# Second layer's input projection by seven block products of summed operands in place of eight, in a two-layer fp32 trunk on one core

## The chip, the core and the metric

The kernel runs on one core of a Trainium2 chip. The core has a matrix engine (PE, TensorE; its weight loads are listed as PEld), a vector engine (DVE), a scalar engine (ACT), a third elementwise engine (POOL, GpSimd) and a queue that issues transfers (SP). Each engine takes its instructions in the order in which they stand; semaphores hold one engine until another is done. SBUF holds operands in 128 partitions; PE writes to PSUM, which has eight banks of 512 fp32 columns.

The metric is the device time of one execution in microseconds (us). Three runs of the kernel before took 918.66, 919.13 and 919.36 us; the median is 919.13.

## The reference

Two residual layers over 512 tokens of 1024 channels, in fp32. The first (even) layer has mLSTM heads and stick-breaking attention; the change leaves what it computes alone. The second (odd) layer is this:

```python
def odd_layer(x, pre_g, post_g, w_in, pool_w, pool_scale, w_out):
    h = rmsnorm(x, pre_g)
    u = h @ w_in                                   # (512, 1024) @ (1024, 4096)
    p, z = u[..., :2048], u[..., 2048:]
    pooled = multiscale_pool(p in 4 groups)        # windows 2, 4, 8, 16
    mixed = einsum('bsgc,gce->bsge', pooled, pool_w) * pool_scale
    y = (mixed * silu(z)) @ w_out
    return x + rmsnorm(y, post_g)
```

The change is in `h @ w_in`.

## The kernel before

**Exact products in three.** PE multiplies in a reduced fp32 form, so every operand is cut in two exact parts: `split` (L70) writes the high half on ACT and the low half, source minus high half, on DVE. A product is then three matmuls, high by high, high by low and low by high (`mm3`, L93). The normed tokens stand transposed as `hTh` and `hTl`, 128 channels by 8 by 512 tokens.

**The odd layer** (L624 to L729) goes through four groups, one for each window (2, 4, 8, 16). For a group it loads the weights of four column tiles of p, 256 columns to a transfer (`col_load`), splits each tile's weights (1024 elements a partition) and multiplies: `col_proj` (L188) runs 8 channel blocks by 3 matmuls of 128x512 for each tile. Group 0 does this in two halves of 256 tokens, since the last tokens of the first layer come late. ACT copies each result out of PSUM; DVE forms window sums (L684), divides, subtracts (L689 to L691) and splits the result into `pph` and `ppl`. Then follow four column tiles of z (`project2`, with Silu on the way out into `sz`), and the group's 512 by 512 map `mx` (L706), whose result DVE scales and multiplies by `sz` into `y32`. After the fourth group comes the output projection `oq` (L537).

**What sets the order.** The program is written in the order above and a scheduler of the framework interleaves it: it chooses each engine's order when the program is built, from its own estimate of durations. Buffers come from rings: `w32` (2 buffers, weights as they come), `wh` and `wl` (4 each, their halves), PSUM banks `pj`, `sc`, `ac` (2 each), `xa` and `xb` (1 each). A ring's next buffer is free when the last reader of its old content is done.

**Names in this text.** `p20` is the first pair of column tiles of p in group 2, `z21` the second pair of z there, `pw` a group's map weights, `mx` its products. `finish_even` (L640) ends the first layer for a tile of 128 tokens and makes the odd layer's normed tokens of it (`prenorm`, L161).

Of the kernel before, what the change touches and what calls it, by code (L numbers as in the profile page):

```python
# [5 lines left out]
F32 = mybir.dt.float32  # L6
# [7 lines left out]
P = 128  # L14
S = 512
# [21 lines left out]
def body(nc, tc, x, pre_g, post_g, w_in, conv, b_i, b_f, hn_g, w_out, w_in_c, pool_w,  # L37
# [6 lines left out]
    with base as base, psum as psum, dram as dram:  # L44
# [10 lines left out]
        # functions that need a table run in the order they are written, so that each  # L55
        # table is loaded once for a run of them
# [21 lines left out]
        def load(parts, a, n, name):  # L78
            """Weights as they come, rows of n columns for each of a row tiles."""
            w32 = base.tile([P, 8 * WIDE // 4], F32, tag="w32", bufs=2, name=f"w32_{name}")  # L80
            w = w32[:, :a * n].rearrange("p (a n) -> p a n", a=a)
            for eng, dst, src in parts(w):
                eng.dma_start(dst, src.rearrange("(a p) n -> p a n", p=P))
            return w

        def halves(w, name, into=None):
            """The two exact parts of a piece of them."""
            a, n = w.shape[1], w.shape[2]
            wh, wl = (t[:, :a * n].rearrange("p (a n) -> p a n", a=a) for t in (into or whl(name)))
            split(w, wh, wl)  # L90
            return wh, wl
# [13 lines left out]
        # the first layer's input and gate rows stand where its output goes later  # L105
# [8 lines left out]
        # constants  # L114
# [21 lines left out]
        # per-channel vectors, one transpose  # L136
# [24 lines left out]
        def prenorm(xt, xs, tt, gain, name, parts=1):  # L161
            ss = base.tile([P, 1], F32, tag="ss", bufs=4, name=f"ss_{name}")
            if parts == 1:
                A.activation(xs, xt, AF.Square, accum_out=ss)
            else:
                s2 = base.tile([P, 2], F32, name=f"s2_{name}")
                for n in range(2):
                    cs = slice(n * 512, n * 512 + 512)
                    A.activation(xs[:, cs], xt[:, cs], AF.Square, accum_out=s2[:, n:n + 1])
                V.tensor_tensor(ss, s2[:, 0:1], s2[:, 1:2], op=ALU.add)  # L170
            r = rstd(ss, name)
            for half in range(2):
                hs = slice(half * 512, half * 512 + 512)
                V.scalar_tensor_tensor(xs[:, hs], xt[:, hs], r, gain[:, hs], op0=ALU.mult,
                                       op1=ALU.mult)
                tp = sc(f"tp{half}_{name}")
                for j in range(4):
                    k = half * 4 + j
                    T.transpose(tp[:, j * P:(j + 1) * P], xs[:, k * P:(k + 1) * P], ident)
                dst = (slice(None), slice(half * 4, half * 4 + 4), slice(tt * P, tt * P + P))  # L180
                split(tp.rearrange("p (a n) -> p a n", a=4), hTh[dst], hTl[dst])

        def col_load(src, name):
            """Two column tiles of an input projection."""
            w = load(lambda t: [(nc.sync, t, src)], 8, 256, name)
            return [lambda i=i: halves(w[:, :, i * P:i * P + P], f"{name}_{i}") for i in range(2)]
# [12 lines left out]
        with tc.tile_pool(name="att", bufs=1) as at:  # L199
# [11 lines left out]
            # first pre-norm, and the values of four heads as its tokens come  # L211
# [206 lines left out]
            class Stick:  # L418
                """One head of stick-breaking attention, key blocks from the last to the first."""
# [120 lines left out]
            def y_split(half, c, tiles, name):  # L540
                """Two channel tiles of y, for one half of the tokens."""
# [82 lines left out]
        with tc.tile_pool(name="odd", bufs=1) as od:  # L624
            def gains(g, name):
                t = od.tile([P, D], F32, tag="gain", bufs=2, name=name)
# [3 lines left out]
            def xs(name): return od.tile([P, D], F32, tag="xs", bufs=2, name=name)  # L630

            def ytiles(n):
                return (od.tile([P, S], F32R, tag="phi", bufs=6, name=f"yh_{n}"),
                        od.tile([P, S], F32R, tag="plo", bufs=6, name=f"yl_{n}"))
# [5 lines left out]
            def finish_even(ps, tt):  # L640
                xt = od.tile([P, D], F32, tag="xt", bufs=2, name=f"xe{tt}")
                nc.sync.dma_start(xt, xr[:, tt])
                t = xs(f"xse{tt}")
                post(ps, t, gpo, xt, xn[:, tt], f"e{tt}")
                prenorm(xn[:, tt], t, tt, gpr, f"p1{tt}")
# [7 lines left out]
            gpo1 = gains(post_g[1], "g_post1")  # L653
            for g, w in enumerate(WINDOWS):
                pooled = []
                cur4 = []
                for j in range(4):
# [4 lines left out]
                wj = [w for i in range(2)  # L662
                      for w in col_load(w_in_c[0, :, 512 * g + 256 * i:512 * g + 256 * i + 256], f"p{g}{i}")]
                if g == 0:
                    wj = [w() for w in wj]
                    steps = [(j, wj[j], n) for n in range(2) for j in range(4)]
                else:
                    steps = [(j, wj[j], None) for j in range(4)]
                for j, wt, n in steps:
                    wt = wt() if n is None else wt  # L670
                    n0, n1 = (0, S) if n is None else (256 * n, 256 * n + 256)
                    ps = pj(f"ps_p{4 * g + j}_{n}")
                    col_proj(wt, ps, n0, n1)
                    A.activation(cur4[j][:, 16 + n0:16 + n1], ps[:, n0:n1], AF.Copy)
                for j in range(4):
# [17 lines left out]
                    ph = od.tile([P, S], F32R, tag="phi", bufs=6, name=f"pph{c}")  # L693
                    pl = od.tile([P, S], F32R, tag="plo", bufs=6, name=f"ppl{c}")
# [3 lines left out]
                for j, ps in enumerate(p for i in range(2) for p in project2(  # L698
                        w_in_c[0, :, 2048 + 512 * g + 256 * i:2304 + 512 * g + 256 * i], f"z{g}{i}")):
                    c = 4 * g + j  # L700
                    t = od.tile([P, S], F32, tag="sz", bufs=6, name=f"sz{c}")
                    act(t, ps, AF.Silu)
                    sz.append(t)
# [10 lines left out]

            outr = out[0].rearrange("(a p) d -> p a d", p=P)

            def finish_odd(ps, tt):
                t, q = xs(f"xo{tt}"), od.tile([P, D], F32, tag="xt", bufs=2, name=f"xq{tt}")
# [37 lines left out]
```

## Time and profile before

| what | value |
|---|---|
| median of three runs | 919.13 us |
| span of the profiled execution, first to last instruction (the only time recorded of that execution) | 916.9 us |
| mean granted PE clock | 0.994 |
| first z product to first `oq` matmul | 621.8 to 814.85 us |
| output projection of the odd layer | to 910 us |
| the last rows of the odd layer behind it | 910 to 916.9 us |

A row of the grouped views reads: line, engine, operation, output <- inputs by the program's names, partitions x elements, count | busy us and mean ns of one | idle time of the engine before it and what ended it. A row of the timeline reads: start, duration, engine, line, operation; in brackets the idle time before it and its releaser. A row of windows reads: stretch and its length, then busy time (and count) by engine, the granted clock of PE as a share of full speed, the share of time in which transfers ran, and GB/s.

### The profile page before, as it was taken

What the parts mean: (1) busy time and instruction counts of PE and PEld (TensorE: products, weight loads), DVE (VectorE), ACT (ScalarE), POOL (GpSimd) and SP (SyncE); (2) the same over time, 40 slices, a digit from 0 to 9 for tenths busy, and PEclk for the clock granted to TensorE, in tenths of its full rate; (3) what the DMA queues carried; (4) which work ended last, traced back from release to release, by engine and by line L of the source; (5) the groups of instructions that cost most, each with busy time, mean ns of one, the idle gap of its engine ahead of it and who ended that gap; (6) DMA issues with size and microseconds to landing.
All of it is one profiled execution on the core that took longest, in us unless ns stands there. A gap on an engine that the chain in (4) does not pass through costs nothing.

```text
span 916.9 us, 11439 instructions
## 1 busy us (share of the span) xinstructions
PE 904.5 (99%) x4453; PEld 759.6 (83%) x4453; DVE 533.8 (58%) x817; ACT 461.5 (50%) x766; POOL 51.9 (6%) x189
## 2 busy tenths in 40 slices
PE   8999999999999999999999999999999999999996
PEld 6788889889988898898898878898888888888885
DVE  5435556567876675764764828665462745737542
ACT  6426666766668464464565536553231422335331
POOL 2001111101101101001000000000000000000000
PEclk8999999999999999999999999999999999999999
DMA  8231321212122332324221456624223333326331
GB/s 299 84 101 49 91 85 54 88 51 82 59 92 90 129 93 95 98 78 133 92 87 52 158 183 229 204 78 136 92 91 93 92 92 92 98 87 229 114 115 47
DMA packets 67126, 98.88 MB, mean 108 GB/s; under 512 B 2848, under 2 KB 54136, under 8 KB 67072
## 3 DMA queue, kind: packets, MB, share of 16 engines
q1 hardware_dynamic: 65888, 98.08, 32.9%
q8 instruction: 35, 0.57, 0.3%
q10 hardware_dynamic: 1184, 0.08, 0.1%
q14 instruction: 19, 0.16, 0.1%
HBM read 96.02 MB, written 2.13 MB: 107 GB/s over the span
## 4 chain that ended last, share of the span: by engine, by line
PE 97%; DMA 1%; DVE 1%; ACT 0%; issue 0%; DVEq 0%; POOL 0%; POOLq 0%
PE op L537 10%; PE oq L537 10%; PE ps_z L97 3%; PE ps_qa L97 3%; PE ps_qa L95 3%; PE ps_qa L96 3%; PE ps_z L95 3%; PE ps_z L96 3%; PE ps_p_None L96 2%; PE ps_p_None L95 2%; PE ps_p_None L97 2%; PE psv_va L95 2%; PE psv_va L97 2%; PE psv_va L96 2%; PE ps_zb L95 2%; PE mx L97 2%
## 5 line engine op out<-in xcount | busy, mean ns | idle before, releaser
L97 PE MATMUL ps_qa<-hTh,wl_qa 128*128 128x512 f32 x128 | 50.3, 393 | 0.0
L95 PE MATMUL ps_qa<-hTh,wh_qa 128*128 128x512 f32 x128 | 50.2, 393 | 0.0
L97 PE MATMUL ps_z<-hTh,wl_z 128*128 128x512 f32 x128 | 50.2, 393 | 0.0
L96 PE MATMUL ps_qa<-hTl,wh_qa 128*128 128x512 f32 x128 | 50.2, 392 | 0.0
L95 PE MATMUL ps_z<-hTh,wh_z 128*128 128x512 f32 x128 | 50.2, 392 | 0.0
L96 PE MATMUL ps_z<-hTl,wh_z 128*128 128x512 f32 x128 | 50.2, 392 | 0.0
L71 ACT ACTIVATE wh_p<-w_p 128x1024 fp32r<-128x1024 f32 x16 | 17.0, 1059 | 60.9 <-PE mx L96 31.9
L72 DVE TENSOR_TENSOR wl_wo_e<-w_wo_e,wh_wo_e 128x1024 fp32r<-128x1024 f32 x28 | 34.2, 1232 | 21.9 <-ACT wh_wo_e L71 21.9
L71 ACT ACTIVATE wh_wo_e<-w_wo_e 128x1024 fp32r<-128x1024 f32 x28 | 29.3, 1058 | 30.3 <-DMA w_wo_e<-in_w_out_ab 15.6
L72 DVE TENSOR_TENSOR wl_p<-w_p,wh_p 128x1024 fp32r<-128x1024 f32 x16 | 19.6, 1223 | 35.1 <-ACT wh_p L71 35.1
L537 PE MATMUL op<-wl_wo_e,yh_e 128*128 128x512 f32 x120 | 39.0, 396 | 0.0
L537 PE MATMUL op<-wh_wo_e,yl_e 128*128 128x512 f32 x120 | 38.8, 395 | 0.0
L537 PE MATMUL op<-wh_wo_e,yh_e 128*128 128x512 f32 x120 | 37.8, 396 | 0.0
L95 PE MATMUL ps_p_None<-hTh,wh_p 128*128 128x512 f32 x96 | 37.7, 393 | 0.0
L96 PE MATMUL ps_p_None<-hTl,wh_p 128*128 128x512 f32 x96 | 37.7, 393 | 0.0
L97 PE MATMUL ps_p_None<-hTh,wl_p 128*128 128x512 f32 x96 | 37.7, 392 | 0.0
L67 ACT ACT_TABLE_LOAD x28 | 35.9, 1283 | 1.3 <-PEq L742 0.8
L97 PE MATMUL psv_va<-wh_va,hTl 128*128 128x256 f32 x128 | 36.1, 282 | 0.0
L95 PE MATMUL psv_va<-wh_va,hTh 128*128 128x256 f32 x128 | 36.1, 282 | 0.0
L96 PE MATMUL psv_va<-wl_va,hTh 128*128 128x256 f32 x128 | 36.1, 282 | 0.0
L317 DVE SCALAR_TENSOR_TENSOR cv<-u,vecs,cv 128x511 f32<-128x511 f32 (+2 forms) x48 | 35.4, 748 | 0.4
L72 DVE TENSOR_TENSOR wl_wo_o<-w_wo_o,wh_wo_o 128x1024 fp32r<-128x1024 f32 x20 | 24.2, 1223 | 18.9 <-ACT wh_wo_o L71 18.9
(310 smaller groups left out, 2659.7 us busy)
## 6 DMA issues: line engine op xcount, KB each, us to landing
w_wo_e<-in_w_out_ab SPq DMA_DIRECT2D x14, 1024.0 KB, 4.9
w_wo_o<-in_w_out_c SPq DMA_DIRECT2D x12, 1024.0 KB, 4.7
w_qa<-in_w_in_ab SPq DMA_DIRECT2D x8, 1024.0 KB, 5.0
w_p<-in_w_in_c SPq DMA_DIRECT2D x8, 1024.0 KB, 5.4
w_z<-in_w_in_c SPq DMA_DIRECT2D x8, 1024.0 KB, 5.4
w_qb<-in_w_in_ab SPq DMA_DIRECT2D x4, 1024.0 KB
w_kb<-in_w_in_ab SPq DMA_DIRECT2D x4, 1024.0 KB, 5.0
w_zb<-in_w_in_ab SPq DMA_DIRECT2D x4, 1024.0 KB, 4.9
```

The source lines that it names most:

```text
L67: link(A.preload_act_table_set(TABLE[func]))
L71: A.activation(hi, src, AF.Copy)
L72: V.tensor_tensor(lo, src, hi.bitcast(F32), op=ALU.subtract)
L95: T.matmul(dst, lhsT=ah, rhs=bh, start=first, stop=False, **kw)
L96: T.matmul(dst, lhsT=ah, rhs=bl, start=False, stop=False, **kw)
L97: T.matmul(dst, lhsT=al, rhs=bh, start=False, stop=last, **kw)
L317: V.scalar_tensor_tensor(acc[:, j:], u[:, :S - j], cw(3 - j, c), acc[:, j:], op0=ALU.mult, op1=ALU.add)
L537: T.matmul(ps[a][n], lhsT=l[:, ta], rhs=r[:, 0, n * 512:n * 512 + 512], start=(first and l is yh and r is wh), stop=(last and l is yl))
```

## The change

A pair of column tiles (256 columns of `w_in`) and the 512 tokens are cut in two by two blocks: channels 0 to 511 and 512 to 1023, first and second column tile, tokens 0 to 255 and 256 to 511. Eight block products become seven, by Strassen's scheme in Winograd's form:

- `hidden_sums` forms four combinations of token blocks once (`d3`, `d1`, `n2`, `t4`, each 128x1024, on DVE) and splits each. They need the normed tokens unsplit, so `prenorm` now also copies each transposed tile into `y32` (ACT, 128x512, eight copies).
- `strassen2` forms four sums of weight blocks for each pair (`s1` to `s4`, each 128x512, on POOL), and splits `a` (first column tile, 1024), `b` and `c` (the sums, 1024 each) and `d` (the fourth weight block, 512). Each of seven products is 4 channel blocks by 3 matmuls of 128x256.
- Partial results are added where they are made: PSUM bank `psa` runs on through four products and is read after each (`pt1`, `pt2`, an output, an output), `pse` through two, `psb` holds one. Three of the reads are copies on ACT, three are additions on DVE, the last is an ACT copy or Silu.
- Group 0's p tiles stay as they were; 14 pairs use the scheme (z of group 0, p and z of groups 1 to 3).
- Rings: gains, squares and input tiles share one ring `big` of 8 with the split token sums; `phi`, `plo` 5 in place of 6, `sz` 4 in place of 6, a new ring `ws` of 3 for the sums; the last gain is loaded after the groups. Two small window operations go from DVE to POOL.

```diff
-        def prenorm(xt, xs, tt, gain, name, parts=1):
+        def prenorm(xt, xs, tt, gain, name, parts=1, keep=None):
...
-                split(tp.rearrange("p (a n) -> p a n", a=4), hTh[dst], hTl[dst])
+                tp = tp.rearrange("p (a n) -> p a n", a=4)
+                split(tp, hTh[dst], hTl[dst])
+                if keep is not None:
+                    A.activation(keep[:, half * 4:half * 4 + 4], tp, AF.Copy)
...
+            def quarter(k, n): return y32[:, 8 * n + 4 * k:8 * n + 4 * k + 4, 0:256]
+            hs = {"11": hblock(0, 0), "21": hblock(1, 0), "22": hblock(1, 1)}
+            def ws(name): return od.tile([P, 8, P], F32, tag="ws", bufs=3, name=name)
+            def hidden_sums():
+                raw = {}
+                b11, b21, b12, b22 = quarter(0, 0), quarter(1, 0), quarter(0, 1), quarter(1, 1)
+                for n in ("d3", "d1", "n2", "t4"):
...
+                    if n == "d3":
+                        V.tensor_tensor(raw[n], b22, b12, op=ALU.subtract)
+                    elif n == "d1":
+                        V.tensor_tensor(raw[n], b11, b12, op=ALU.subtract)
+                    elif n == "n2":
+                        V.scalar_tensor_tensor(raw[n], raw["d3"], -1.0, b11, op0=ALU.mult, op1=ALU.subtract)
+                    else:
+                        V.scalar_tensor_tensor(raw[n], raw["n2"], -1.0, b21, op0=ALU.mult, op1=ALU.subtract)
+                    split(raw[n], *hs[n])
+            def strassen2(src, name, dsts, silu=False):
+                w = load(lambda t: [(nc.sync, t, src)], 8, 256, name)
+                a11, a12, a21, a22 = (w[:, 4 * k:4 * k + 4, m * P:m * P + P]
+                                      for m in range(2) for k in range(2))
+                sums = [ws(f"ws{i}_{name}") for i in range(2)]
+                s1, s2, s3, s4 = sums[0][:, 4:], sums[0][:, :4], sums[1][:, :4], sums[1][:, 4:]
+                G.tensor_tensor(s1, a21, a22, op=ALU.add)
+                G.tensor_tensor(s2, s1, a11, op=ALU.add)
+                G.tensor_tensor(s3, a11, a21, op=ALU.add)
+                G.tensor_tensor(s4, a12, s2, op=ALU.add)
+                first = halves(w[:, :, :P], f"{name}_a")
+                second = halves(sums[0], f"{name}_b")
+                third = halves(sums[1], f"{name}_c")
+                fourth = halves(a22, f"{name}_d")
...
+                pa, pb, pe = (f(f"ps{n}_{name}")[:, :256] for f, n in ((pj, "a"), (xa, "b"), (xb, "e")))
+                product(pa, first, 0, "11", True, True)
+                A.activation(t1, pa, AF.Copy)
+                product(pb, first, 4, "21", True, True)
+                V.tensor_tensor(dsts[0][:, :256], pb, t1, op=ALU.add)
+                product(pa, second, 0, "n2", False, True)
+                A.activation(t2, pa, AF.Copy)
+                product(pe, second, 4, "d1", True, True)
+                A.activation(t5, pe, AF.Copy)
+                product(pa, third, 0, "d3", False, True)
+                V.scalar_tensor_tensor(dsts[1][:, 256:], pa, -1.0, t5, op0=ALU.mult, op1=ALU.subtract)
+                product(pe, third, 4, "22", False, True)
+                V.tensor_tensor(dsts[0][:, 256:], pe, t2, op=ALU.add)
+                product(pa, fourth, 0, "t4", False, True)
...
-                    V.tensor_tensor(sm[:, :e], sm[:, :e], invc[:, :e], op=ALU.mult)
-                    V.tensor_tensor(sm[:, :e], sm[:, :e], p32[:, :e], op=ALU.subtract)
+                    G.tensor_tensor(sm[:, :e], sm[:, :e], invc[:, :e], op=ALU.mult)
+                    G.tensor_tensor(sm[:, :e], sm[:, :e], p32[:, :e], op=ALU.subtract)
```

How it changes the engines' orders is shown at three places. First DVE at the start of the z products of group 0, before (`wl_z00_0` and `wl_z00_1` are the low halves of the two column tiles of the first z pair):

```order
L72 TENSOR_TENSOR hTl_64<-tp1_p13_5460,hTh_63 128x4x128
L72 TENSOR_TENSOR wl_z00_0_5745<-w32_z00_5741,wh_z00_0_5744 128x1024
L684 TENSOR_TENSOR p_0_1_5705<-p_0_5469 128x512
L72 TENSOR_TENSOR wl_z00_1_5777<-w32_z00_5741,wh_z00_1_5776 128x1024
L684 TENSOR_TENSOR p_1_1_5714<-p_1_5471 128x512
```

and now, from the same last row of normed tokens:

```order
L72 TENSOR_TENSOR hTl_64<-tp1_p13_5467,hTh_63 128x4x128
L679 TENSOR_TENSOR raw_d3_5711<-y32_65 128x1024
L681 TENSOR_TENSOR raw_d1_5717<-y32_65 128x1024
L683 SCALAR_TENSOR_TENSOR raw_n2_5723<-raw_d3_5711,y32_65 128x1024
L72 TENSOR_TENSOR d3l_5713<-raw_d3_5711,d3h_5712 128x1024
L72 TENSOR_TENSOR d1l_5719<-raw_d1_5717,d1h_5718 128x1024
L72 TENSOR_TENSOR wl_z00_a_5782<-w32_z00_5773,wh_z00_a_5781 128x1024
L685 SCALAR_TENSOR_TENSOR raw_t4_5729<-raw_n2_5723,y32_65 128x1024
L762 TENSOR_TENSOR p_0_1_5735<-p_0_5475 128x512
L72 TENSOR_TENSOR n2l_5725<-raw_n2_5723,n2h_5724 128x1024
L762 TENSOR_TENSOR p_1_1_5744<-p_1_5477 128x512
L769 SCALAR_TENSOR_TENSOR p_0_1_5735<-p_0_1_5735,p_0_5475 128x511
```

The token sums and their low halves stand ahead of and between the weight splits; `t4l` and then `wl_z00_b`, the low half of the first pair of weight sums, are the next two rows of 1024.

Second, POOL at the same place, where before it only cleared window edges:

```order
L660 MEMSET p_0_5469 128x16
L660 MEMSET p_1_5471 128x16
L660 MEMSET p_2_5473 128x16
L660 MEMSET p_3_5475 128x16
L660 MEMSET p_4_5936 128x16
```

and now, with the sums of z00 (`ws0` is b: s2 and s1; `ws1` is c: s3 and s4) and then of z01:

```order
L695 TENSOR_TENSOR ws0_z00_5775<-w32_z00_5773 128x512
L696 TENSOR_TENSOR ws0_z00_5775<-ws0_z00_5775,w32_z00_5773 128x512
L767 TENSOR_TENSOR p_0_1_5735<-p_0_1_5735,invc_101 128x1
L768 TENSOR_TENSOR p_0_1_5735<-p_0_1_5735,p_0_5475 128x1
L697 TENSOR_TENSOR ws1_z00_5776<-w32_z00_5773 128x512
L698 TENSOR_TENSOR ws1_z00_5776<-w32_z00_5773,ws0_z00_5775 128x512
L767 TENSOR_TENSOR p_1_1_5744<-p_1_1_5744,invc_101 128x1
L695 TENSOR_TENSOR ws0_z01_5901<-w32_z01_5899 128x512
L768 TENSOR_TENSOR p_1_1_5744<-p_1_1_5744,p_1_5477 128x1
L697 TENSOR_TENSOR ws1_z01_5902<-w32_z01_5899 128x512
L696 TENSOR_TENSOR ws0_z01_5901<-ws0_z01_5901,w32_z01_5899 128x512
```

POOL now has work of 128x512 for every pair, in between operations that DVE waits for.

Third, DVE in group 2 between the p and the z products, before:

```order
L72 TENSOR_TENSOR wl_p21_1_6413<-w32_p21_6320,wh_p21_1_6412 128x1024
L72 TENSOR_TENSOR wl_z20_0_6506<-w32_z20_6502,wh_z20_0_6505 128x1024
L684 TENSOR_TENSOR p_8_1_6442<-p_8_6310 128x512
L684 TENSOR_TENSOR p_8_2_6445<-p_8_1_6442 128x512
L684 TENSOR_TENSOR p_8_4_6448<-p_8_2_6445 128x512
```

and now:

```order
L725 TENSOR_TENSOR p_8_6702<-pse_p20_6736,pt2_p20_6738 128x256
L762 TENSOR_TENSOR p_8_1_6952<-p_8_6702 128x512
L72 TENSOR_TENSOR wl_p21_c_6848<-ws1_p21_6834,wh_p21_c_6847 128x1024
L762 TENSOR_TENSOR p_8_2_6955<-p_8_1_6952 128x512
L717 TENSOR_TENSOR p_10_6706<-psb_p21_6856,pt1_p21_6858 128x256
L72 TENSOR_TENSOR wl_p21_d_6852<-w32_p21_6831,wh_p21_d_6851 128x512
L762 TENSOR_TENSOR p_8_4_6958<-p_8_2_6955 128x512
L72 TENSOR_TENSOR wl_z20_a_7023<-w32_z20_7014,wh_z20_a_7022 128x1024
L769 SCALAR_TENSOR_TENSOR p_8_4_6958<-p_8_4_6958,p_8_6702 128x505
L762 TENSOR_TENSOR p_9_1_6967<-p_9_6704 128x512
L72 TENSOR_TENSOR wl_z20_b_7027<-ws0_z20_7016,wh_z20_b_7026 128x1024
L723 SCALAR_TENSOR_TENSOR p_11_6708<-psa_p21_6855,pt5_p21_6860 128x256
```

Each pair now has four splits and three reads out of PSUM on DVE, and the window sums stand between them.

More of the change, by code (lines that the diff above doesn't have):

```diff
@@ L651, in body, with hblock @@
                       lambda a: finish_even(ps1[a], 2 + a))
-            gpo1 = gains(post_g[1], "g_post1")
+            def quarter(k, n): return y32[:, 8 * n + 4 * k:8 * n + 4 * k + 4, 0:256]
+            def hblock(k, n):
+                ix = (slice(None), slice(4 * k, 4 * k + 4), slice(256 * n, 256 * n + 256))
+                return hTh[ix], hTl[ix]
+            hs = {"11": hblock(0, 0), "21": hblock(1, 0), "22": hblock(1, 1)}
+            def ws(name): return od.tile([P, 8, P], F32, tag="ws", bufs=3, name=name)
@@ L697, in body @@
                 sz = []
[L698 to L703, printed above, removed]
+                for i in range(2):
+                    pair = [od.tile([P, S], F32, tag="sz", bufs=4, name=f"sz{4 * g + 2 * i + j}")
+                            for j in range(2)]
+                    strassen2(w_in_c[0, :, 2048 + 512 * g + 256 * i:2304 + 512 * g + 256 * i],
+                              f"z{g}{i}", pair, True)
+                    sz.extend(pair)
                 w4 = load(lambda t: [(nc.sync, t, pool_w[0, g])], 4, 512, f"pw{g}")
@@ L740 @@
     from concourse.bass_utils import run_bass_kernel_spmd as _run
[L742 removed]
+    nc = _bacc.Bacc("TRN2", target_bir_lowering=False, num_devices=1,
+                    dynamic_dma_scratch_size=1024)
     arrays, args = {}, []
```

59 lines of the change are left out of this document (37 added, 22 removed).

## The prediction

> **What bounds the kernel now.** I read the page first: busy times, the row of PE by slices, and the head of the chain that ended last.
>
> ```profile
> PE 904.5 (99%) x4453; PEld 759.6 (83%) x4453; DVE 533.8 (58%) x817; ACT 461.5 (50%) x766; POOL 51.9 (6%) x189
> PE   8999999999999999999999999999999999999996
> PE 97%; DMA 1%; DVE 1%; ACT 0%; issue 0%; DVEq 0%; POOL 0%; POOLq 0%
> ```
>
> The chain runs through PE for 97% of its length, and no slice but the first and last shows PE below nine tenths. So PE sets the time, and a matmul less is worth its pace. The pace is not the "mean ns of one", since matmuls overlap; it is start to start, which the chain shows where one line runs unbroken, and the timeline of PE where the pieces are single:
>
> ```profile
> 823.01 86.96 PE oq L537 x373
> ```
> ```profile
> 604.61 0.28 PE L95 MATMUL ps_p<-hTh,wh_p 128*128 128x256 f32 x1
> ...
> 607.00 0.28 PE L97 MATMUL ps_p<-hTh,wl_p 128*128 128x256 f32 x1
> ```
>
> A matmul with 512 moving columns costs 86.96/373 = 0.233 us; the second pair are the first and the last of 21 rows of 256 columns with a weight load of its own each: 2.39/20 = 0.1195 us. Half the columns cost 51%, so the products of 256 columns lose almost nothing.
>
> The stage of the change, by windows (span, then PE, PEld, DVE, ACT and POOL busy):
>
> ```profile
> 621.80:814.80 193.00, 193.00 (x837) 157.08 (x837) 98.37 (x145) 60.74 (x82) 4.01 (x36) 1.00 0.31 96
> ```
>
> Before, DVE works 98 of 193 us here, ACT 61, POOL 4. All of the slack that the change can spend is in this row, and it adds to all three.
>
> **The change part by part. 1. Matmuls removed.** A pair of column tiles had 48 matmuls of 512: 11.2 us. It now has 7 products of 12, so 84 of 256: 10.04 us. That is 1.17 us for each of 14 pairs (2 in group 0, 4 in each other group): **-16.4 us**, all on the path.
>
> **2. Prices of what is added on DVE.** The timeline of DVE gives busy times and, from one start to the next, what the engine really needs:
>
> ```profile
> 614.60 1.23 DVE L72 TENSOR_TENSOR wl_z<-w_z,wh_z 128x1024 fp32r<-128x1024 f32 x1 [4.92 <-ACT wh_z L71]
> 615.74 0.69 DVE L684 TENSOR_TENSOR p<-p 128x512 f32<-128x512 f32 x1
> 616.34 1.22 DVE L72 TENSOR_TENSOR wl_z<-w_z,wh_z 128x1024 fp32r<-128x1024 f32 x1
> ```
>
> 1.14 us for 1024 columns, 0.60 for 512. A pair's low halves were two of 1.14; now they are a, b, c (1.14 each) and d (0.60), and three additions out of PSUM of 256 columns. ACT's part (three more splits' worth and three copies a pair) stays inside its slack: 61 us of 193 before, and some 2.5 us more for each of 14 pairs.
>
> **3. POOL, and what it does to DVE.** Each pair also gets four sums of 128x512 on POOL. Before, POOL adds only in the mLSTM stage, at shorter lengths. The timelines of POOL and of DVE, first where DVE left it alone:
>
> ```profile
> 413.37 1.01 POOL L381 TENSOR_TENSOR w<-w,w 128x384 f32<-128x384 f32 x1 [45.28 <-DVE pl L72]
> 418.04 0.74 POOL L381 TENSOR_TENSOR w<-w,w 128x256 f32<-128x256 f32 x1 [3.66 <-DVE w L367]
> 420.27 0.46 POOL L381 TENSOR_TENSOR w<-w,w 128x128 f32<-128x128 f32 x1 [1.21 <-DVE w L367]
> 412.82 0.55 DVE L72 TENSOR_TENSOR pl<-w,ph 128x384 fp32r<-128x384 f32 x1
> ```
>
> 0.46, 0.74, 1.01: 0.275 us for each 128 columns, so 1.29 us for 512 (an estimate from these rows). Then two places where both had work:
>
> ```profile
> 297.02 1.02 POOL L381 TENSOR_TENSOR w<-w,w 128x384 f32<-128x384 f32 x1 [13.21 <-DVE pl L72]
> 299.09 1.58 POOL L381 TENSOR_TENSOR w<-w,w 128x256 f32<-128x256 f32 x1 [1.05 <-DVE w L367]
> ```
> ```profile
> 297.20 1.25 DVE L72 TENSOR_TENSOR pl<-w,ph 128x384 fp32r<-128x384 f32 x1 [0.34 <-ACT ph L71]
> 298.52 0.42 DVE L367 SCALAR_TENSOR_TENSOR w<-s,w 128x256 f32<-128x256 f32 x1
> 298.86 1.22 DVE L72 TENSOR_TENSOR wl_qa<-w_qa,wh_qa 128x1024 fp32r<-128x1024 f32 x1
> 299.99 0.96 DVE L72 TENSOR_TENSOR pl<-w,ph 128x256 fp32r<-128x256 f32 x1
> 300.88 0.28 DVE L367 SCALAR_TENSOR_TENSOR w<-s,w 128x128 f32<-128x128 f32 x1
> ```
>
> At 297.20 DVE starts a 384 that takes 1.25 instead of 0.55 and ends 0.4 after POOL. At 299.09 POOL's 256 takes 1.58 instead of 0.74: it stands still until DVE's split of 1024 is over, and then DVE's next, a 256 that should need 0.42 as the row at 298.52, stands still in its turn (0.96). They take turns, one whole instruction each; the one held back loses about the other's length less 0.2 us: 0.70 of the 0.84 us that POOL still had at 297.20, 0.54 of 0.74 at 299.99. So where DVE always has work with both operands in SBUF, a sum of 512 costs DVE 1.29 - 0.2 = **1.09 us**. Bounds: 0 if it falls into DVE's gaps, 1.29 if all of it counts. I take 1.09, since DVE will have no gaps in the stretches below. DVE's reads out of PSUM (0.35 us by 298.52 to 298.86) may run beside a sum.
>
> [...]
>
> **4. Groups 1 to 3.** Take in group 2 the stretch from the end of p20's sixth product to the first mx. PE has 208 matmuls of 256: 24.9 us. DVE has, in the order of the changed program, 8 operations of 1024 (low halves c of p21, a, b, c of z20 and z21, first of the pool weights), 19 of 512 (d of three pairs, window sums, pooled low halves) and 7 out of PSUM: 9.1 + 11.4 + 2.5 = 23.0 us, after 0.6 for the PSUM read that has to wait for that sixth product: 23.6. Alone that just fits. But the eight sums of z20 and z21 fall here: z20's weights can be fetched only when d of p20 is split, and land, 5.4 us later, at the start of the stretch.
>
> ```profile
> w_z<-in_w_in_c SPq DMA_DIRECT2D x6, 1024.0 KB, 5.4
> ```
>
> 8 x 1.09 = 8.7 us make 32.3 for 24.9: DVE is 7.4 us late at the first mx. It cannot have worked ahead, since four pieces of weights are all that the ring holds. PE meets the lateness in parts, at the PSUM reads that free psb and psa (the same banks serve the next product) and at wl of z20, z21 and pool weights. Less about 0.6 for PSUM reads beside a sum: 6.8 us. Group 1 has the same counts: 6.8. Group 3 has two window sums more: 8. Behind the first mx PE has mx and the first half of the next pair, and DVE little; nothing is lost there, and nothing regained, for PE was full before. Together **+21 us** (bounds: 0 with sums free, 26 with 1.29).
>
> **5. Group 0.** Around the last pre-norm ACT, DVE and PE stood so (timelines of the three):
>
> ```profile
> 607.76 1.09 ACT L71 ACTIVATE hTh<-tp_p 128x512 fp32r<-128x512 f32 x2
> ```
> ```profile
> 608.39 1.29 DVE L72 TENSOR_TENSOR hTl<-tp_p,hTh 128x512 fp32r<-128x512 f32 x2 [0.93 <-ACT hTh L71]
> ```
> ```profile
> 609.13 0.39 PE L96 MATMUL ps_p<-hTl,wh_p 128*128 128x256 f32 x1 [0.22 <-DVE hTl L72]
> ```
>
> Two of the copies into y32 (0.55 us each by the first row) now stand on ACT ahead of these, and hold the PSUM banks of the transposes: **+0.4 us**. The two for the last tile come behind, so d3 starts on DVE at about 610.5. To the low half b of z00 DVE has 10 operations of 1024 and 3 of 512: 13.2 us, to 623.7. PE, from 609.5, has 96 + 24 matmuls of 256 before it needs that: 623.8. Again a fit without POOL; the four sums of z00 are 4.4 us, so PE waits about 4.5 us. Then to low half c: 3.3 us of DVE against 3.4 of PE, and the four sums of z01 on top: 4.4 again. Two waits: **+9 us** (bounds 0 and 11).
>
> **6. At nothing:** small window edges moved from DVE to POOL (0.07 us each on DVE), fewer buffers in the rings phi, plo and sz (four of each are live at a time, and five, five and four are left; where one came short, a split would wait for one mx of 12, 2.8 us), the later load of the gain (its first reader is some 45 us on), the tail (same rows in both orders). Not one moves the end unless DVE is early.
>
> **Sum:** -16.4 + 0.4 + 21 + 9 = +14 on a span of 916.9, so 930.9. The median of the runs, 919.13, is 2.2 above that span, and I keep the distance: **933 us**.
>
> **Rivals.** *The sums fit in (not slower).* POOL's sums cost DVE nearly nothing, since DVE waits for ACT and PE between splits in any case: the row of the stage gives DVE 95 idle us of 193. Then -16.4 + 0.4 and some 2.5 us of new waits in PE's order: 905.6. One price decides: with b per sum the waits are about 8b in group 0 and 8b less spare 1.3, 1.3 and 0.1 in the others; 32b - 2.7 reaches 16 at b = 0.58 us. Against it stand the collisions of part 3, where DVE lost 0.54 and 0.70 to shorter sums.
>
> *Half of it.* Sums and DVE's PSUM reads and gaps overlap more than I count, b about 0.6: the gain is eaten and no more, 914 to 924.
>
> *The clock drops as well.* The two waits of group 0 are over 4 us each. The windows show the granted clock (third from the right) where PE ends:
>
> ```profile
> 910.00:916.90 6.90, 0.00 (x0) 0.00 (x0) 2.34 (x5) 0.97 (x3) 0.00 (x0) 0.73 0.21 77
> ```
>
> If idle PE goes from 1 to half speed, a mean of 0.73 over 6.9 us says that it did so after some 3.2 us. A wait of 4.5 us would then cross it; if the clock takes as long to come back, 3.2 us at half speed lose 1.6 us after each wait, 3 in all: 936. With the whole 1.29 for every sum (32 x 0.2 = 6 us) it is 942, so 938 to 946 for this case. [...]
>
> *That the matmuls do not shrink* is out: the order of the changed program has 504 more rows on PE, which is 14 x (84 - 48).
>
> **How the numbers follow.** Forecast (waits of 24 to 33 us, 926 to 938) 0.58; clock or whole instructions (938 to 946) 0.10; half (914 to 924) 0.14; fit (903 to 914) 0.18. About 0.2% (1.8 us) can be told from no change: faster 0.18 and a fifth of "half", 0.21; same 0.06; slower 0.73. The range 912 to 940 leaves out most of the fit and the top.
>
> **What would show it.** Right: PE's idle before z00's second products in two pieces of about 4 us, with wl_z00 and DVE as releasers; PE waiting in each later group for DVE (evictions out of psa and psb, wl_z, wl_pw); DVE's splits of 1024 above 1.22 us in the mean, near 2 us where a sum runs; POOL's sums at 1.3 us or, behind a split, up to 2.4. Matmuls of 256 in the products still 0.12 us apart where nothing waits. Wrong: splits at 1.22 us throughout and PE unbroken, which is the fit; or ACT as the releaser of PE, which I costed at nothing.

## The result, and the profile after

The changed kernel takes **934.9 us** in the median (931.9 to 938.0, four runs) against 919.25 us of the kernel before, run beside it: a ratio of 1.0168, 95% interval 1.0144 to 1.0191. The change makes the kernel 1.7% slower. The forecast was 933 us, with a range of 912 to 940.

First the page of the changed kernel: the busy line, the row of PE by slices, and the clock by slices.

```profile
PE 903.9 (97%) x4957; PEld 783.1 (84%) x4957; DVE 603.9 (65%) x863; ACT 503.3 (54%) x850; POOL 170.4 (18%) x277
PE   8999999999999999999999999988989999889997
PEclk8999999999999999999999999998989999989998
```

PE no longer fills its row: slices 27, 28, 30, 35 and 36 fall below nine tenths, and the granted clock falls in three slices there (28, 30, 36). POOL went from 51.9 to 170.4 us. The head of the chain says nothing this time, since it could be followed back only to the last mx.

The windows, group by group (stretch and length, busy PE, PEld, DVE, ACT and POOL, then clock):

```profile
605.00:651.00 46.00, 39.63 (x277) 37.60 (x276) 38.01 (x41) 25.81 (x43) 23.71 (x21) 0.89 0.14 45
651.00:703.00 52.00, 47.63 (x332) 45.19 (x332) 37.92 (x45) 20.46 (x33) 30.55 (x32) 0.93 0.26 83
703.00:760.00 57.00, 55.14 (x411) 52.18 (x410) 42.70 (x52) 28.02 (x46) 28.64 (x29) 1.00 0.30 93
760.00:831.00 71.00, 63.43 (x454) 59.09 (x453) 59.23 (x73) 35.02 (x56) 39.95 (x42) 0.99 0.36 113
```

PE idles 6.4, 4.4, 1.9 and 7.6 us in groups 0 to 3. DVE is not busy all the time in any of these rows; it is so in the short stretches where PE waits for it, as the next views show. Whom PE waits for in this stage (waits in us, number, longest):

```profile
PE psa_z L97 <- DVE wl_z_a L72: 8.1, 4, 2.8
PE mx L95 <- ACT pph L71: 3.3, 1, 3.3
PE psb_z L95 <- DVE p L717: 3.3, 3, 1.6
PE pse_z L95 <- ACT wh_z_b L71: 2.4, 1, 2.4
PE psb_z L95 <- DVE sz L717: 1.4, 2, 0.8
```

The longest item is the low half a of the second z pair of a group, four times; then evictions of psb, which free the bank for the next pair; both by DVE. Two waits end with ACT, and neither stands so in the forecast, which had named ACT as the releaser of PE among its signs of being wrong.

What a sum on POOL does to DVE, from both timelines (POOL first):

```profile
627.80 2.27 POOL L698 TENSOR_TENSOR ws_z<-w_z,ws_z 128x512 f32<-128x512 f32 x1
632.93 1.28 POOL L697 TENSOR_TENSOR ws_z<-w_z 128x512 f32<-128x512 f32 x1
```
```profile
628.85 1.76 DVE L769 SCALAR_TENSOR_TENSOR p<-p,p 128x511 f32<-128x511 f32 x1
632.84 0.41 DVE L717 TENSOR_TENSOR sz<-psb_z,pt_z 128x256 f32<-128x256 f32 x1
633.17 2.12 DVE L72 TENSOR_TENSOR wl_z_c<-ws_z,wh_z_c 128x1024 fp32r<-128x1024 f32 x1
```

The sum at 627.80 stands still behind a split of DVE (2.27 where 1.28 is its free length); then DVE's own operation of 511 columns takes 1.76 instead of 0.68: it is held for 1.08 us, against the 1.09 of the forecast. The eviction out of PSUM at 632.84 runs beside a sum at its normal 0.41 (all 14 reads of psb in this trace took 0.409 to 0.425); the split of 1024 behind it needs 2.12 instead of 1.22. The forecast looked for splits near 2 us, and they are there.

The early part of the program, which the change does not touch, differs by up to 3.7 us between profiled runs (the last `op` matmul starts at 592.6 to 596.3). From there to the last `oq` matmul it is 315.0 us before and 333.7 after, 18.7 more; with the 16.4 us of matmuls saved, PE comes 35.1 us late in this execution, the slowest of the four (938.0 us).

### The profile page after: what moved, and what is told of

Read it like the earlier page. It is cut to its first block, busy times and chain, and to the rows that moved or that the text cites. A ratio compares the mean times of both kernels' runs of the same rounds, so it can differ in the third digit from the quotient of the medians.

```text
span 936.3 us, 12756 instructions
## 1 busy us (share of the span) xinstructions
PE 903.9 (97%) x4957; PEld 783.1 (84%) x4957; DVE 603.9 (65%) x863; ACT 503.3 (54%) x850; POOL 170.4 (18%) x277
## 5 line engine op out<-in xcount | busy, mean ns | idle before, releaser
L762 DVE TENSOR_TENSOR p<-p 128x512 f32<-128x512 f32 x40 | 37.9, 955 | 0.1
L384 POOL TENSOR_TENSOR w<-w,w 128x384 f32<-128x384 f32 (+2 forms) x12 | 10.4, 869 | 144.8 <-DVE pl L72 135.9
L67 ACT ACT_TABLE_LOAD x28 | 35.9, 1283 | 1.3 <-PEq L821 0.8
L695 POOL TENSOR_TENSOR ws_z<-w_z 128x512 f32<-128x512 f32 x8 | 17.8, 2229 | 98.6 <-DVE d1l L72 69.0
L447 POOL TENSOR_SCALAR_AFFINE_SELECT a<-a 128x128 f32<-128x128 f32 x32 | 12.1, 387 | 126.9 <-DVE a L445 111.3
L72 DVE TENSOR_TENSOR wl_qa<-w_qa,wh_qa 128x1024 fp32r<-128x1024 f32 x16 | 19.6, 1222 | 18.4 <-ACT wh_qa L71 18.4
L540 PE MATMUL oq<-wl_wo_o,yh_o 128*128 128x512 f32 x96 | 31.3, 405 | 0.0
L540 PE MATMUL oq<-wh_wo_o,yh_o 128*128 128x512 f32 x96 | 31.3, 404 | 0.0
L71 ACT ACTIVATE wh_wo_o<-w_wo_o 128x1024 fp32r<-128x1024 f32 x20 | 20.9, 1053 | 19.2 <-PE oq L540 8.1
```

Of the source, the lines that this page charges most:

```text
L67: link(A.preload_act_table_set(TABLE[func]))
L71: A.activation(hi, src, AF.Copy)
L72: V.tensor_tensor(lo, src, hi.bitcast(F32), op=ALU.subtract)
L384: G.tensor_tensor(total[:, t0:], total[:, t0:], w[:, t0:], op=ALU.add)
L447: G.affine_select(a[:, t0:t0 + P], a[:, t0:t0 + P], pattern=[[1, P]], base=-1, channel_multiplier=-1, compare_op=ALU.is_ge, fill=0.0)
L540: T.matmul(ps[a][n], lhsT=l[:, ta], rhs=r[:, 0, n * 512:n * 512 + 512], start=(first and l is yh and r is wh), stop=(last and l is yl))
```

## The experiments

Every experiment is an edit of the changed kernel. The change also sets the program's dynamic DMA scratch to 1024, which its description leaves out. The experiments keep that setting, so none of them tests it; weights of z land 5.3 us after their issue in the changed kernel and 5.4 before.

The scheduler may order a program anew after an edit. The kernels without sums and with unread sums have the same order on PE, DVE and ACT in their traces, so their difference is clean. Against the changed kernel theirs differs in group 0, and with the sums on DVE many more operations change places.

**No sums.** b and c are split from the weights as they came; all else stands.

```diff
-                G.tensor_tensor(s1, a21, a22, op=ALU.add)
...
-                second = halves(sums[0], f"{name}_b")
+                second = halves(w[:, :, P:], f"{name}_b")
```

> The four sums of each pair on POOL are gone; the halves b and c are split from a part of the weights as they came (the sums of the weights are left out of the computation). Matmuls, splits, evictions and additions as many as in the changed kernel. Theory (sums on POOL hold DVE up): PE waits in the stage for 2 to 5 us in all, granted clock back at 0.99, 904 to 909 us. Rival (DVE has too much of its own, sums or not): DVE late all the same, PE waits over 12 us, 918 to 930. Rival (sums and DVE's load share it by halves): 912 to 918.

**Sums that nobody reads.** The four sums stay on POOL, and b and c are split as in the kernel without sums.

> POOL makes the same four sums of 128x512 a pair, but nothing reads them: b and c are split from a part of the weights (the sums are left out of what follows). Theory (the sums cost DVE time by collision): DVE's splits beside a sum still take 1.75 and 2.1 us, PE waits 12 to 20 us, 922 to 934 us. Rival (the sums cost nothing on DVE that matters, it is that b and c come late behind them): PE as without sums, 904 to 909.

**POOL busy, but without reading SBUF.** Four memsets in place of the four sums.

```diff
-                G.tensor_tensor(s1, a21, a22, op=ALU.add)
...
+                for part_sum in (s1, s2, s3, s4):
+                    G.memset(part_sum, 0.03)
```

> In place of the sums four memsets of 128x512 on POOL, b and c split from them (the weights' sums are left out of the computation): POOL has as many instructions at the same places, and b and c wait for POOL, but POOL reads nothing from SBUF. Theory (two readers of SBUF exclude each other): DVE's splits at their free length (0.68 and 1.22 us), 904 to 910 us. Rival (any work on POOL holds DVE up): splits at 1.75 and 2.1 us, 922 to 934. Rival (waiting for POOL as such): splits free, but PE waits for halves b and c, 915 to 925.

**Sums on DVE.** `V.tensor_tensor` in place of `G.tensor_tensor` for all four.

> The same four sums, on DVE. Each should take 0.60 us from start to start (0.68 busy) in place of 1.29 on POOL and about 1.09 of DVE's time held. Theory (price on DVE 1.09 on POOL, 0.60 on DVE): the waits of groups 1 to 3 shrink by 8 x 0.49 = 3.9 us a group, those of group 0 by some 4: 916 to 921 us. Rival (the sums on POOL were mostly hidden, DVE alone is the bound): DVE gets 2.4 us a pair more, slower than the changed kernel, 938 to 950.

Measured, one after the other: 912.0 us without sums (ratio 0.9919, interval 0.9898 to 0.9939), **931.9** with unread sums (1.0136, 1.0116 to 1.0157), 914.3 with memsets (0.9947, 0.9928 to 0.9966), 921.1 with the sums on DVE (1.0022, 1.0012 to 1.0032). The unread sums came out as expected, and the sums on DVE at the upper end of what was expected. The other two missed: 912.0 lies above the 904 to 909 of its theory, at the edge of the rival "by halves", and 914.3 above 904 to 910. In both PE waits 3.3 us at the last mx, which is treated below.

DVE's operations grouped by line and shape, in the stage, as columns count | busy us, mean ns: first the unread sums, then no sums, memsets, sums on DVE.

```profile
L762 DVE TENSOR_TENSOR p<-p 128x512 f32<-128x512 f32 x40 | 37.7, 949 | 0.1
L72 DVE TENSOR_TENSOR wl_z_c<-w_z,wh_z_c 128x1024 fp32r<-128x1024 f32 x8 | 12.5, 1568 | 0.1
```
```profile
PE 892.8 (98%) x4957; PEld 775.0 (85%) x4957; DVE 577.2 (63%) x863; ACT 502.9 (55%) x850; POOL 75.7 (8%) x221
L756 DVE TENSOR_TENSOR p<-p 128x512 f32<-128x512 f32 x40 | 27.1, 685 | 0.2
```
```profile
L72 DVE TENSOR_TENSOR wl_z_c<-ws_z,wh_z_c 128x1024 fp32r<-128x1024 f32 x8 | 9.8, 1223 | 3.2 <-ACT wh_z_c L71 3.0
L696 POOL MEMSET ws_z<- 128x512 f32 x32 | 15.8, 525 | 113.4 <-DVE d1l L72 68.9 <-DVE wl_p_c L72 30.4 <-DVE wl_p_b L72 14.0
```
```profile
L762 DVE TENSOR_TENSOR p<-p 128x512 f32<-128x512 f32 x40 | 27.1, 684 | 0.4 <-POOL p L768 0.3
```

The same 40 window additions take 949 ns each beside sums that nobody reads and 685 without them; the low half c 1568 ns against 1223 beside memsets. So it is neither work on POOL as such nor the waiting for POOL's result that holds DVE up. What is left is POOL's reading of SBUF: beside it the operations with both operands there (`p<-p`, `wl_z_c<-w_z,wh_z_c`) are longer, and the eviction at 632.84, with one operand in PSUM, keeps its 0.41 us. By what mechanism is not shown. In time, unread sums cost 2.2% of the kernel before (1.0136 against 0.9919), some 20 us; that b and c also wait for them (the step from 1.0136 to 1.0168) costs 3 us more, an estimate from two sets of runs whose intervals overlap, and group 0 has another order there. In the memset run DVE idles 3.0 us for the high half c, and its 2 us over the run without sums fit that.

All DVE operations together are 26.7 us longer in the changed kernel than without sums (603.9 less 577.2). Spread over the 32 sums of the z pairs that is 0.83 us a sum, not 1.09. Laid beside POOL's rows, some 25 us of it stand beside sums of z pairs and 2 beside sums of p pairs. On DVE the sums cost more of its time than they did from POOL (page: DVE 610.3 us), and yet the kernel is 14 us faster so. If the price of a z sum falls from 0.83 to about 0.60, that is 32 x 0.23 = 7 us, and the 3 us for lateness may go as well. This split is an estimate, since the order on DVE changed too; about 4 us of the 14 I cannot assign.

**p pairs alone.** The z pairs are projected by 48 matmuls as before, the p pairs of groups 1 to 3 by seven products, sums on POOL.

> Seven products for the p pairs of groups 1 to 3 alone (6 pairs of 14), the sums on POOL as in the change; the z pairs by 48 matmuls as before. Theory (a sum costs PE time only where DVE has no room): 6 x 1.17 = 7.0 us less of matmuls, half of DVE's added load and no sums in the z stretch, PE waits under 2 us: 911 to 915 us. Rival (each sum on POOL costs about the same wherever it stands): the added time of 14 pairs in proportion, 6/14 of +16, 924 to 928.

915.7 us, ratio 0.9962 (0.9948 to 0.9975): faster than before, a little less than expected, and far from the rival. PE's longest wait in the stage is 0.8 us. Of the 7.0 us of matmuls 3.2 arrive, so the six pairs' sums, splits and reads cost 3.8 us at most, where 14 pairs cost 32.

**The clock.** Behind several waits the matmuls stand wider apart, as in this piece of PE's timeline of the changed kernel, and the windows give the granted clock (third from the right):

```profile
696.58 0.58 PE L97 MATMUL psa_z<-hTh,wl_z_a 128*128 128x256 f32 x1 [2.76 <-DVE wl_z_a L72]
696.96 0.41 PE L95 MATMUL psa_z<-hTh,wh_z_a 128*128 128x256 f32 x1
...
702.30 0.41 PE L96 MATMUL pse_z<-hTl,wh_z_c 128*128 128x256 f32 x1
```
```profile
696.00:700.00 4.00, 3.42 (x16) 3.42 (x17) 4.00 (x7) 0.82 (x2) 1.73 (x4) 0.50 0.60 221
```

From 696.96 to 702.30 there are 25 steps in 5.34 us, 0.2136 each where 0.1195 is the pace. There are four such stretches, 8.6 us of delay in all (2.4, 1.6, 2.5 and 2.1). I had priced them only in a rival. Two kernels fill waits with matmuls into a bank that nobody reads, bound to their place by an order without a semaphore; the first is the one with sums on DVE.

```diff
+        def fill(n, name, last):
+            ps = sc(f"fill_{name}")
+            for k in range(n):
+                i = T.matmul(ps[:, :256], lhsT=hTh[:, k % 4, :P], rhs=hTh[:, k % 4, :256],
+                             start=k == 0, stop=k == n - 1, skip_group_check=True)
+                after(i, last)
+                last = i
+            return last
```

> The kernel with the sums on DVE, and 44 idle-time matmuls of 256 columns into an unused bank ahead of the second products of z00, 28 about the first mx of the last group; all other instructions stand in the same order. They take the room of two waits (3.2 us and 3.3 us) after which the matmuls stood 0.213 us apart instead of 0.1195. Theory (the granted clock falls since PE waited): no stretch at half clock behind these two places, granted clock 0.99 in the mean, 4 to 5 us less than the sums on DVE without it, 916 to 917.5 us. Rival (the clock falls for another reason, as load): the stretches stay, 921 us or more.

919.2 us, ratio 1.0001 (0.9991 to 1.0011), about 2 us better than without filling, half of what was expected. The windows of group 0, sums on DVE without and with filling:

```profile
625.00:640.00 15.00, 10.00 (x55) 9.50 (x54) 14.65 (x22) 7.37 (x11) 5.20 (x13) 0.66 0.23 65
```
```profile
625.00:640.00 15.00, 14.31 (x118) 13.90 (x117) 14.65 (x22) 8.24 (x13) 5.98 (x13) 1.00 0.17 53
```

The clock goes from 0.66 to 1.00 with the same other work: the waits bring it down. From the last transposes to the end of z00's product d it saves 2.3 us (35.9 to 33.6). At the last mx the filling saved hardly anything: behind the last z product PE is as late as before by the engines it waits for. Then the changed kernel itself:

> The changed kernel itself with matmuls of 256 columns into an unused bank in three of its waits: 20 ahead of the second products of z00, 20 ahead of the first low half of z01, 26 ahead of the first mx of the last group. The three stretches at half clock behind them cost 2.4, 1.6 and 2.1 us in the profiled run. Theory (waits bring the clock down, and that costs the time by itself): these stretches go, granted clock 0.99; in group 0 about 4 us less, at the last mx little, since it is late by the window sums: 929 to 931.5 us. Rival (the clock's loss lies beside the same lateness of DVE and is given back): 933 to 937.

934.8 us, ratio 1.0164 (1.0149 to 1.018): no gain at all. In its profiled run the mean clock is 0.991, in that of the changed kernel 0.981. In the order of the fences, the changed kernel and the filled one, the last transposes of the pre-norm and the last matmul of the last z pair:

```profile
608.91 0.55 PE L179 MATMUL tp_p<-ident,xse 128*128 128x128 f32 x3 [0.31 <-ACT y L184]
...
826.41 0.28 PE L97 MATMUL psa_z<-t4h,wl_z_d 128*128 128x256 f32 x1
```
```profile
606.30 0.66 PE L193 MATMUL tp_p<-ident,xse 128*128 128x128 f32 x4 [0.31 <-ACT y L198]
...
823.84 0.28 PE L99 MATMUL psa_z<-t4h,wl_z_d 128*128 128x256 f32 x1
```

217.50 us and 217.54 us. Of 23.9 us at half clock in this stage 13.7 are left, partly behind other waits, and the end did not move by 0.1 us. That is what the rival said: DVE is late, and the slow matmuls use up time that PE would have waited for it. It is not shown cleanly, though. PE's order in group 0 differs between the two, and the 20 matmuls ahead of z01 themselves ran at half clock (3.64 us for a wait of 2.45), so that z01's product d ended 2.0 us later. And over the four runs of the changed kernel time and clock go together, from 931.9 us at 0.991 to 938.0 us at 0.981. Whether the clock costs this kernel time by itself stays open.

**Ten, eleven, twelve pairs.** With sums on DVE, the z pairs of some groups go back to 48 matmuls: of groups 0 and 3 (ten pairs by seven products), of group 0 alone (twelve), and of group 3 and z00 (eleven); last, the ten pairs with their sums on POOL.

```diff
+                    if g in (0, 3):
+                        for t, ps in zip(pair, project2(zsrc, f"z{g}{i}")):
+                            act(t, ps, AF.Silu)
+                    else:
+                        strassen2(zsrc, f"z{g}{i}", pair, True)
```

> Sums on DVE, seven products for ten pairs (p and z of groups 1 and 2, p of group 3); z of groups 0 and 3 by 48 matmuls. Theory: 10 x 1.17 = 11.7 us less, groups 1 and 2 without waits as with all sums on DVE, no late low half in group 0, and the last mx not late as DVE has less to do in group 3 and PE more; 0.4 for the copies: 907 to 910 us. Rival (the last mx waits in this order as well, with the clock): 911 to 914.

> Sums on DVE, seven products for twelve pairs (all of groups 1 to 3); z of group 0 by 48 matmuls. Theory: 12 x 1.17 = 14.0 us less, no wait in group 0, but the first mx of the last group waits about 3.4 and 1.7 us and a stretch at half clock follows it (2 us), 0.4 for the copies: 911 to 914 us. Rival (that wait went with group 0's lateness): 905 to 908.

> The ten-pair version with its sums on POOL in place of DVE. Theory (a sum on POOL holds DVE for about its length, and only the z pairs of groups 1 and 2 stand where DVE has no room): the waits of these two groups as in the changed kernel, 4.9 and 2.4 us, with a stretch at half clock of 2.5 us: 918 to 922 against 911 with the sums on DVE. Rival (POOL's sums cost mainly in group 0 and at the end): 910 to 914.

> The ten-pair version with z01 of group 0 by seven products as well (eleven pairs, sums on DVE). Theory: 1.17 us less of matmuls; DVE has half of group 0's added splits and sums, and z00 by 48 matmuls covers them: 909 to 910.5. Rival (z01's halves come late as z00's did): 912 to 915.

Ten pairs: 910.95 us, ratio 0.9911 (0.9896 to 0.9926), just above the 907 to 910 of the theory, though PE waits nowhere for more than 0.4 us. Eleven: **909.7 us, 0.9897 (0.9882 to 0.9911)**, faster than both kernels. Ten with sums on POOL: 919.4 us, 1.0004 (0.9993 to 1.0015), as expected; where the sums run is worth 8.5 us, with the change of order that comes with it, and nearly all of it falls in groups 1 and 2. The windows of these two groups, sums on POOL, then on DVE:

```profile
651.00:700.00 49.00, 44.62 (x331) 42.85 (x330) 38.54 (x45) 23.12 (x37) 18.75 (x25) 0.97 0.27 86
700.00:760.00 60.00, 57.08 (x417) 53.62 (x416) 47.11 (x57) 27.79 (x45) 34.00 (x36) 1.00 0.32 102
```
```profile
651.00:700.00 49.00, 49.00 (x373) 47.01 (x372) 40.21 (x60) 25.00 (x40) 9.23 (x17) 1.00 0.34 108
700.00:760.00 60.00, 59.63 (x447) 56.77 (x446) 53.95 (x81) 30.21 (x49) 14.17 (x20) 1.00 0.29 88
```

PE idles 7.3 us in the one and 0.4 in the other. Twelve pairs missed the expectation: 918.3 us (0.9990, 0.9979 to 1.0001) where 911 to 914 were expected. PE waits 4.7 us at the last group's mx. ACT and DVE before it:

```profile
802.06 2.00 ACT L71 ACTIVATE wh_wo_o<-w_wo_o 128x1024 fp32r<-128x1024 f32 x2 [3.63 <-DMA w_wo_o<-in_w_out_c]
805.17 1.28 ACT L67 ACT_TABLE_LOAD   x1
806.47 0.63 ACT L71 ACTIVATE pph<-p 128x512 fp32r<-128x512 f32 x1
```
```profile
803.15 1.23 DVE L72 TENSOR_TENSOR wl_wo_o<-w_wo_o,wh_wo_o 128x1024 fp32r<-128x1024 f32 x1 [2.13 <-ACT wh_wo_o L71]
804.29 0.67 DVE L769 SCALAR_TENSOR_TENSOR p<-p,p 128x497 f32<-128x497 f32 x1
```

The halves of the output projection's first weights stand ahead of the pooled half that mx needs, on both engines, and wait for a transfer until 802.06; a table load comes on top. The engines are not overloaded here, they stand in the wrong order. The test moves just that:

```diff
+            late["A"], late["V"] = third_split
...
+        def behind(i, eng):
+            if eng in late:
+                tc.add_manual_dep(i.ins, late[eng].ins.name, NOSYNC, reason="behind pooled")
+            return i
```

> The twelve-pair version with one thing moved: the first two pieces of the output projection's weights (their halves on ScalarE and VectorE) and the table load stand behind the pooled halves of the third column tile of the last group, not ahead of them; PE's order is the same. In the run without it these stood in front while their transfer was on the way (ACT idle 3.6 us, then 2.0 + 1.3 us of work; VectorE idle 2.1 us), and the first mx waited 4.7 us. Theory (the wait at the last mx comes from this order on ACT and VectorE, not from too much work): the wait falls to under 1 us, no stretch at half clock, 6 to 8 us less than the twelve pairs without it: 910 to 913 us. Rival (VectorE's window sums are late by their number): 916 to 919.

911.5 us, ratio 0.9916 (0.9902 to 0.9929), 7 us less than without the move:

```profile
799.45 0.62 ACT L78 ACTIVATE pph<-p 128x512 fp32r<-128x512 f32 x1
799.98 2.00 ACT L78 ACTIVATE wh_wo_o<-w_wo_o 128x1024 fp32r<-128x1024 f32 x2
801.99 1.28 ACT L67 ACT_TABLE_LOAD   x1
```

The pooled half is there at 800.1, and the wait at the third tile is down to 0.4 us; one of 1.9 us is left at the fourth, where under 1 was expected. A stretch at half clock still follows that one, from 803.96 to 807.37, against 10.2 us of it in the run without the move; none was expected.

## Why the prediction was right

The time came out 2 us above the forecast, and its main cause was the one named. That it came so close is partly luck: groups 1 to 3 were forecast 8 us too high, against 5.4 us for the tail and some 7 us without a place that it did not have. By its steps:

- **Matmuls (-16.4 us).** Right. The counts are as forecast (504 rows more), and where nothing waits the products stand 0.1195 us apart. Versions with six, ten and eleven pairs gain 3.2, 7.9 and 9.6 us where the price gives 7.0, 11.7 and 12.9. The steps between them fit the price roughly; some 3.5 us are lost whatever the number of pairs. The forecast had 0.4 of that, for the copies; where the rest goes stays open.
- **Price of a sum.** The estimate of 1.29 us on POOL was right (1.28 free), and so was the time for which it holds one DVE operation: 1.09 forecast, 1.08 measured. Per z sum, counting those that fall in gaps, it was 0.83. As forecast, DVE's PSUM reads run beside a sum (0.41 us at 632.84).
- **Where it is paid.** In the z stretches and in group 0, as forecast; with p pairs alone PE hardly waits. The alternation I inferred is what the rows show mostly, with one large exception, below.
- **Groups 1 to 3 (+21 us; its parts add to 21.6).** Oversized by 8. Forecast 6.8, 6.8 and 8. PE idles 4.4, 1.9 and 4.3 us (7.6 less the 3.3 at the last mx), and slow matmuls lose 2.5 us more in group 1: 6.9, 1.9 and 4.3, together 13. The term that was off is the price per sum (0.83 for 1.09), and beyond it probably the assumption that DVE had no gap in any of the three; why group 2 loses so much less than group 1 with the same counts stays open.
- **Group 0 (+0.4 and +9 us).** PE idles 6.4 us of the window (0.5 before), and the two stretches at half clock add 4.0: 10. The size was right, the places half so. The first wait was there (2.4 us, then slow matmuls), but by the high half b on ACT, which waited for POOL; the second came at low half a of z01 (2.45 us) and not at c of z00 (0.4 us).
- **The tail, at nothing.** Wrong: 5.4 us. The mx of the last group waits 3.3 us for a pooled half behind weights' halves and a table load on ACT, and slow matmuls behind it lose 2.1. This happens even without sums. The sentence "same rows in both orders" looked at what stands there, not at what now stands in front of what. The twelve-pair test shows this order to be the cause there; in the changed kernel ACT's rows have the same order, but it was not moved in that kernel itself.
- **The rival "the sums fit in"** was given 905.6 us. With no sums at all the kernel takes 912.0: I left out 6 us, mainly the wait at the last mx and its slow matmuls (3.3 and 1.9 us in that trace). Of the 32 us that the changed kernel takes beyond 919.2 - 16.4, some 20 come from collisions, 3 from sums read late, and 9 are there without any sum, over half of them at the last mx.
- **The rival "the clock drops as well".** The clock did drop, after waits of 2.4 to 3.3 us and not only over 4. With sums on DVE that cost 2.3 us in group 0; here filling the waits gained nothing, and whether its cost is to be added stays open. What failed is that a wait must last some 3.2 us: in the changed kernel's trace the clock changes in steps of 3.41 us, and a wait of 2.4 us inside one step was enough (last section); PE was still busy for 28 to 43% of the four steps before a fall. The rival's upper part, the whole 1.29 us for every sum, no run shows: the operation at 628.85 lost 1.08 us to a sum of 1.28, and the mean is 0.83.
- **What no row shows.** The named pieces (10, 13 and 5.4) make 28.4 of the 35.1 us. Since the row of a matmul is 0.16 us longer than its step (0.28 against 0.1195), each of some 20 waits hides that much, 3 us; the rest is in stalls too short to read.

## What to carry to other kernels

Work given to an idle engine was not free here, since it held up the engine that is late next: a POOL addition of 1.28 us out of SBUF cost a busy DVE 1.08 us (0.83 a sum in the mean), and doing it on DVE was cheaper (921.1 against 934.9 us). Use the scheme where the engine that feeds it has room (eleven pairs of fourteen, 1% faster than before) and not where it fills that engine's last gaps. When a stage gets shorter, look at what now stands in front of its last inputs on in-order engines: one move of two weight pieces and a table load was worth 7 us.

## What the hardware showed beyond the forecast

The turns between POOL and DVE are not always taken. In the changed kernel the first sum of z00 waits through a whole run of DVE operations (POOL, DVE and ACT):

```profile
617.44 7.41 POOL L695 TENSOR_TENSOR ws_z<-w_z 128x512 f32<-128x512 f32 x1 [68.98 <-DVE d1l L72]
```
```profile
617.27 1.22 DVE L72 TENSOR_TENSOR wl_z_a<-w_z,wh_z_a 128x1024 fp32r<-128x1024 f32 x1
...
622.49 1.22 DVE L72 TENSOR_TENSOR t4l<-raw_t,t4h 128x1024 fp32r<-128x1024 f32 x1
627.32 1.61 DVE L72 TENSOR_TENSOR wl_z_b<-ws_z,wh_z_b 128x1024 fp32r<-128x1024 f32 x1 [3.61 <-ACT wh_z_b L71]
```
```profile
626.23 1.06 ACT L71 ACTIVATE wh_z_b<-ws_z 128x1024 fp32r<-128x1024 f32 x1 [5.41 <-POOL ws_z L696]
```

It takes 7.41 us where 1.28 is its free length: it got its turn only when DVE's unbroken run was over at 623.7, and no operation of that run was longer than its free length. DVE then idles 3.61 us for b, whose sums came late, so the first wait of group 0 is POOL held by DVE and not the other way about. In the kernel with unread sums the same sum took 2.20 us behind one operation; what decides whether POOL gets in between two operations of DVE stays open.

The granted clock of the changed kernel's trace changes only on a grid of 3.41 us. In the stage it is 0.50 from 627.50 to 634.33, 641.15 to 644.57, 695.77 to 702.59 and 828.89 to 835.71, one or two steps each; from one of these eight edges to the next it is 2, 2, 1, 15, 2, 37 and 2 times 3.413 us. With sums on DVE a stretch of three steps occurs (627.41 to 637.65, 10.24 us). The step before the third stretch, the stretch, the step behind it, and one step that brought no fall:

```profile
692.36:695.77 3.41, 1.47 (x13) 1.26 (x11) 3.41 (x3) 1.33 (x2) 2.46 (x3) 1.00 0.31 41
695.77:702.59 6.82, 6.01 (x28) 6.01 (x29) 5.83 (x9) 1.01 (x2) 2.98 (x9) 0.50 0.37 135
702.59:706.00 3.41, 3.41 (x30) 3.41 (x30) 2.95 (x5) 3.19 (x6) 0.00 (x0) 1.00 0.00 0
804.99:808.41 3.42, 2.13 (x16) 1.96 (x16) 3.42 (x4) 1.33 (x2) 2.78 (x4) 1.00 0.23 38
```

In the four steps before these falls PE was busy for 28, 29, 35 and 43%; steps with 53% (678.71 to 682.12) and 62% (the last row) brought none. So it should matter where on the grid a wait lies, which no run tested. No threshold follows: in the filled changed kernel one fall came after a step with 67%. Matmuls of 256 columns step at 0.2136 us in such a stretch, 1.79 times the normal pace.
